# Two of four frame columns turned by VectorE by way of memory, and a pooled split kept back until the next pair of products

## Chip, cores and metric

The kernel runs on one core of one Trainium2 chip. The metric is its time on the device in microseconds (us), lower is better; the time before is the median of three executions. One more execution was taken with the hardware profiler, and all rows below are from it.

The core's engines run side by side, each through its own list of instructions in order: TensorE (PE in the rows; PEld is its weight load) multiplies, VectorE (DVE) and ScalarE (ACT) work element by element, GpSimd (POOL) does small things and issues some of the transfers (DMAs), SyncE (SP) issues most of them. They wait for each other through semaphores. An instruction that waits holds up all that stand behind it in its engine's list.

## What is computed

One layer over 2048 prompt frames and 32 sample frames of 1024 channels, cut to what matters here:

```python
hn = rmsnorm(h, g_mix)
proj = hn @ w_in                                     # 1024 x 3072
hA, bA, cA, zA, vB, zB = jnp.split(proj, ...)        # 512 columns each
u = cA * hA
yA = bA * (causal depthwise conv of u, width 3, + bias) * silu(zA)
yB = ((trailing mean of vB over 2/4/8/16 frames - vB) @ pool_w) * pool_scale * silu(zB)
h = h + concat(yA, yB) @ w_out
h = h + (p @ w_ple) * sigmoid(rmsnorm(h, g_ple) @ w_ple_gate)
return rmsnorm(h, g_final), ...
```

The change lies in the first two lines: in how the normalized frames hn are brought into the layout that the product with w_in needs, and in one step of yB.

## The kernel before

**Products.** Each float32 operand is split into two parts (`split`, L76: ScalarE casts the high part, VectorE subtracts it to get the low part), and a product takes three matmuls per block of 128 channels: high x high, high x low, low x high. The third needs the low half of the weight.

**Frames and groups.** The 2080 frames are five blocks of 416 (`NB`). `GROUPS` puts blocks 0 and 1 in group 0, 2 and 3 in group 1, block 4 in group 2. For groups 0 and 1 the product with w_in is done in seven half products in place of eight (`seven`, L894, and `pair`, L854): sums and differences of frames, called 11, 21, T1, T2, T3, 22 and T4, against sums and differences of weights, called 11, 12, S2, S1, S3, S4 and 22. A *product* below is one of these seven, 12 matmuls of 128 x 416.

**Units and pairs.** A *unit* is a group and one of four slices j of the 512 columns. From unit 1 of group 0 on a unit has three *pairs* of kinds of columns, zb with v, c with h, za with b, of seven products each, in the order 11, 12, S2, S1, S3, S4, 22. Three PSUM banks X, Y, Z belong to a pair (rows name them x_ch, y_ch, z_ch and so on). Between products ScalarE copies a bank out (`carry`, L866: into zs, V, c_s, U) or VectorE adds it (`out`, L869), and the next product into that bank waits for it. Weight tiles (`wtile`) have seven buffers, so a pair's weights are split while the pair before is multiplied. VectorE does the low half of each.

**Pooling.** When a zb/v pair is done, `v_first` (L908) copies the last bank into V and calls `pool_blocks` (L730): VectorE forms windowed sums (win) and pl, then the pooled frames are split into pp at L759. `mix` (L718) multiplies pp by the pool weights (pm) behind the c/h pair; in unit 0 of group 1, where two pairs run side by side, within the third pair.

**Frames of group 1.** While group 0's units 1 to 3 run, `next_columns` (L1038) prepares group 1's frames beside them, in the steps of a generator. Four columns c are done in the order 3, 0, 1, 2: columns 0 to 2 are two tiles of 128 frames (one of each block), column 3 is one tile of 64 (32 of each block). For a column `frame_sums` (L436) does this: the sum of squares of each tile (`sumsq`, ScalarE, rows "junk"; POOL makes rstd of it), `normal` (L404, VectorE scales a tile in one operation of 1024), `turn` (L410, four TensorE transposes for each half of each tile into a PSUM bank, rows pt_g), two copies by ScalarE (f12, f21), four subtractions by VectorE, seven splits, each into a *staged tile*, which POOL's queue writes to memory (`to_memory`, L482; p_d). Group 1 reads them back with `load_group`.

**Buffers.** Loaded frame tiles (xt), staged tiles and, where used, the tiles xs and xb named next come from one pool, `xin`, of five buffers of 4 KB a partition, so a load may wait until an older tile has been written out.

**The way through memory.** Block 4 is prepared in group 1 by `last_block` (L1050) without TensorE: `scaled_to_memory` (L1082) scales a tile in four operations of 256 columns into xs and writes it to xs_d, `from_memory` (L1093) loads it back as four pieces into xb, so that each 32 frames by 32 channels stand together, and `turned_in_place` (L1101) turns 32 x 32 blocks in one VectorE operation.

**What sets the order.** A scheduler orders each engine's instructions when the program is built, by its own estimate of times; `keep_in_program_order` binds some of them to the order of the source. `at_pace` (L1106) spreads the steps of a generator over the calls of `aside`, one after each product: 39 steps over 62 calls here.

Of the kernel before, what the change touches and what calls it, by code (L numbers as in the profile page):

```python
# [9 lines left out]
F32 = mybir.dt.float32  # L10
F32R = mybir.dt.float32r
AF = mybir.ActivationFunctionType
ALU = mybir.AluOpType
# [15 lines left out]
KH = KC // 2  # L29
EARLY = 3  # L30
LATE = 2


@with_exitstack
def trunk(ctx, tc, x_p, x_s, c_conv, c_pool, p_p, p_s, g_mix, w_in, conv_w, conv_b, pool_w,
# [294 lines left out]
    with ExitStack() as s1:  # L330
# [140 lines left out]
            yield  # L471


        NAMES = ("11", "21", "T2", "T1", "T3", "22", "T4")
        SLOTS = (("11", "21"), ("T2", "T1"), ("T3", "22"))
        p_d = {q: tc.dram_tile([P, KH, 2, NB], F32, name=f"p_d{q}") for q in NAMES}
# [4 lines left out]

        def to_memory(mem, name, src, at, n, t=None, later=False):  # L482
            t = t or staged(name)[:, :, :, :n]
            ins = put(t, src)
            if later:
                tc.keep_in_program_order(ins)
            nc.gpsimd.dma_start(mem[:, :, :, at:at + n], t.bitcast(F32))
# [185 lines left out]
        class Unit:  # L673
# [53 lines left out]
                nc.vector.scalar_tensor_tensor(z, pm[:, :NB], pscale(j), z, op0=ALU.mult, op1=ALU.mult)  # L727
                self.store(4 + j, b, self.zs)

            def pool_blocks(self, *bs):  # L730

                tb, j, V, L = self.tbs[bs[0]], self.j, self.V, self.L
                win = 2 << j
                if self.pooled is None:
                    self.pooled = wk.tile([P, 2, 2 * NB], F32R, tag="pp", bufs=1, name=f"pp_{self.tag}")
                for seg in self.segs(*bs):
                    lo, hi, at, new = seg
                    m = hi - lo
                    v = self.place(V, 15, seg)

                    src, off = V, (L + 15 if new else 0) + 15 + at
                    step, need = 1, win - 2
                    while step < win:
                        dst = etile(f"win{step}_{self.tag}_{tb}_{new}", 2 * NB + 16)
                        nc.vector.tensor_tensor(dst[:, :m + need], src[:, off - need:off + m],
                                                src[:, off - need - step:off + m - step], op=ALU.add)
                        src, off = dst, need
                        step *= 2
                        need -= step
                    pl = etile(f"pl_{self.tag}_{tb}_{new}", m)  # L750
                    skip = 0
                    if tb == 0:
                        skip = win - 1
                        nc.vector.tensor_tensor(pl[:, :skip], src[:, :skip], cnt[:, first_of(j):first_of(j + 1)],
                                                op=ALU.mult)
                        nc.vector.tensor_tensor(pl[:, :skip], pl[:, :skip], v[:, :skip], op=ALU.subtract)
                    nc.vector.scalar_tensor_tensor(pl[:, skip:], src[:, skip:m], 1.0 / win, v[:, skip:],
                                                   op0=ALU.mult, op1=ALU.subtract)
                    split(self.pooled[:, 0, lo:hi], self.pooled[:, 1, lo:hi], pl)  # L759

            def conv(self, *bs):

# [131 lines left out]
            def seven(self, B, aside, both=False):  # L894
# [12 lines left out]

                def v_first(ps):  # L908
                    nc.scalar.copy(at(V, 15, 0), ps)
                    self.pool_blocks(0, 1)  # L910
                    self.keep(V, 15, halo_v)

                def h_second(ps):
# [19 lines left out]
                def b_first(ps):  # L933
                    mul(self.cols(c_s, 0), ps, self.cols(c_s, 0))
                    self.store(j, 0, c_s)

                ring = [spare_ring if both and i == 1 else raw_ring for i in range(3)]
                pairs = [
                    ("zb", "v", B, {(0, 0): self.cols(zs, 0), (0, 1): self.cols(zs, 1), (1, 1): at(V, 15, 1)},
# [8 lines left out]
                while i < 3:  # L948
                    side_by_side = 2 if both and i == 0 else 1
                    if i <= 1 < i + side_by_side:  # L950
                        self.history(U, 2, halo_u, hist_u(j))
                    steps = [self.pair(*pairs[i + n], ring[i + n], ftile if n else None) for n in range(side_by_side)]
                    for n in range(8):
                        for st in steps:
                            next(st)
                            aside()
                        if both and i == 2 and n == 3:
                            for b in range(2):
                                self.mix(b)
                    for st in steps:  # L960
                        assert next(st, None) is None
                    i += side_by_side
                    if i - side_by_side <= 1 < i and not both:
                        for b in range(2):
                            self.mix(b)
# [72 lines left out]
        def next_columns(*cs):  # L1038

            load_ahead(1, cs[0])  # L1040
            for c, after in zip(cs, cs[1:] + (None,)):

                places = iter(t[:, :, :, i * DEC:(i + 1) * DEC] for t in map(staged, ("short_0", "short_1")) for i in range(4))
                dst = lambda q, src, n: to_memory(p_d[q], f"{q}_1_{c}", src, c * P, n, next(places) if n == DEC else None, True)
                for i, _ in enumerate(frame_sums(ahead.pop((1, c)), f"g1_{c}", dst)):
                    if after is not None and i in (6, 7):
                        load_half_ahead(after)
                    yield

# [27 lines left out]
                    back[c], m = from_memory(c * P, n), n  # L1077
                yield

        xs_d = tc.dram_tile([NB, D], F32, name="xs_d")  # L1080

        def scaled_to_memory(x, r):  # L1082

# [35 lines left out]
        for gi, tbs in enumerate(GROUPS):  # L1119
# [17 lines left out]
            for j in range(4):  # L1137
                unit = gi * 4 + j
                u = Unit(gi, tbs, j)
                if unit == 0:  # L1140
# [1 line left out]
                    B0["T4"] = piece_of(seventh("B0_T4"), 0)  # L1142
                    nc.sync.dma_start(B0["T4"].bitcast(F32), p_d["T4"])
                    p_d["T4"] = tc.dram_tile([P, KH, 2, NB], F32, name="p_dT4b")
                    aside = at_pace(next_columns(3, 0, 1, 2), 39, 62)
                elif gi == 0:
                    u.seven(B, aside)
                elif gi == 1:
# [444 lines left out]
```

## Time and profile before

| What | us |
|---|---|
| median of 3 executions | 927.71 (926.48 to 930.38) |
| the profiled execution, its own time | 928.9 |
| span of its profile | 927.1 |
| TensorE busy | 906.4 (98%) |
| VectorE busy | 722.5 (78%) |
| ScalarE busy | 475.7 (51%) |
| granted TensorE clock, mean | 0.997 |

How to read the rows. A row of the order of time has its start in us from the start of the span, its length in us, engine, line of the kernel, operation, output<-inputs by the program's names (buffer numbers left out), shape and how many like it were merged; in brackets at the end stands how long the engine was idle ahead of it and whose end released it. An instruction's length reaches up to 0.1 us past the start of the next, so prices are taken from start to start. A unit of group 0 takes some 50 us: unit 1 begins at 75.7, unit 2 at 127.3, unit 3 at 182.5, group 1 at 233.8.

### The profile page before, as it was taken

To read this page: it belongs to the slowest core of one execution; us is meant where nothing else is said; L and a number is where in the kernel's file an instruction comes from. 1 tells how busy PE (TensorE), PEld (TensorE's weight loads), DVE (VectorE), ACT (ScalarE), POOL (GpSimd) and SP (SyncE) were. 2 spreads that over 40 slices of the span, in tenths; PEclk is the share of its full clock that TensorE was granted. 3 is DMA by queue.
4 is the path that set the end of the run, shared out by engine and by line. 5 is a ranking of instruction groups with operands and counts; after the bars stand their busy time and mean duration, and the time that the engine had idled before them with its cause. 6 is when DMAs were issued, how large, how long until landed. Compare 5 with 4: busy or idle time off the path is not lost. (4 is left out here: it accounts for less than half of the span.)

```text
span 927.1 us, 12920 instructions
## 1 busy us (share of the span) xinstructions
PE 906.4 (98%) x4479; PEld 817.4 (88%) x4479; DVE 722.5 (78%) x1225; ACT 475.7 (51%) x880; POOL 153.1 (17%) x276
## 2 busy tenths in 40 slices
PE   7999998999999999999999999999999999999996
PEld 5999998999999999999999987888877868888884
DVE  6996998899488989785777678665554799888965
ACT  7743555464345555443545456334334776465554
POOL 4110311212000111000000010111111002333324
PEclk9999999999999999999999999999999999999998
DMA  8344654859955745458665359765785886799882
GB/s 261 91 141 144 188 173 141 246 160 318 413 163 175 198 155 163 119 184 279 180 186 172 128 192 282 251 202 171 245 230 160 299 251 163 187 230 236 224 244 92
DMA packets 140654, 186.37 MB, mean 201 GB/s; under 512 B 12044, under 2 KB 111244, under 8 KB 139309
## 3 DMA queue, kind: packets, MB, share of 16 engines
q1 hardware_dynamic: 120093, 126.07, 44.5%
q0 software_dynamic: 17760, 53.97, 19.8%
q10 hardware_dynamic: 2736, 5.51, 1.8%
q8 instruction: 35, 0.57, 0.3%
q14 instruction: 30, 0.25, 0.1%
HBM read 128.93 MB, written 56.56 MB: 200 GB/s over the span
## 5 line engine op out<-in xcount | busy, mean ns | idle before, releaser
L77 ACT CAST y_S<-y_fS 128x512 fp32r<-128x512 f32 x32 | 19.5, 621 | 42.4 <-PE x_o L167 17.4
L102 PE MATMUL e<-wq,pps 128*128 128x512 f32 (+1 forms) x156 | 38.9, 399 | 0.2 <-ACT pps L77 0.2
L69 POOL TENSOR_SCALAR ms_x<-ssq_x 128x1 f32<-128x1 f32 (+2 forms) x18 | 12.8, 710 | 143.9 <-ACT junk L88 143.6
L167 PE MATMUL x_o<-wo_b,y_S 128*128 128x512 f32 x128 | 35.8, 392 | 0.0
L563 PE MATMUL x_ch<-B,w_ch_S 128*128 128x416 f32 x168 | 34.6, 352 | 1.2 <-ACT c_s L866 1.2
L167 PE MATMUL x_g<-wg_b,g_S 128*128 128x512 f32 x128 | 35.7, 389 | 0.0
L563 PE MATMUL x_zab<-B,w_zab_S 128*128 128x416 f32 x168 | 34.3, 352 | 0.7 <-ACT V L866 0.7
L563 PE MATMUL x_zbv<-B,w_zbv_S 128*128 128x416 f32 x168 | 34.3, 352 | 0.3 <-ACT zs L866 0.3
L563 PE MATMUL z_zbv<-B,w_zbv_S 128*128 128x416 f32 x168 | 34.0, 351 | 0.0
L563 PE MATMUL z_ch<-B,w_ch_S 128*128 128x416 f32 x168 | 34.0, 351 | 0.0
L563 PE MATMUL z_zab<-B,w_zab_S 128*128 128x416 f32 x168 | 34.0, 351 | 0.0
L1382 POOL DMA_DIRECT2D e<-h_d x28 | 24.9, 909 | 53.4 <-DVE e L1379 46.4
L102 PEld LDWEIGHTS e<-wq,pps 128*128 128x128 f32 (+1 forms) x156 | 27.4, 182 | 6.9 <-ACT pps L77 0.5
L563 PEld LDWEIGHTS x_ch<-B,w_ch_S 128*128 128x128 f32 x168 | 31.2, 188 | 1.9 <-ACT c_s L866 1.6
L563 PEld LDWEIGHTS x_zab<-B,w_zab_S 128*128 128x128 f32 x168 | 31.3, 188 | 1.4 <-ACT V L866 1.0
L563 PEld LDWEIGHTS x_zbv<-B,w_zbv_S 128*128 128x128 f32 x168 | 31.2, 188 | 1.1 <-ACT zs L866 0.7
L563 PEld LDWEIGHTS z_ch<-B,w_ch_S 128*128 128x128 f32 x168 | 31.4, 188 | 0.3
L563 PEld LDWEIGHTS z_zab<-B,w_zab_S 128*128 128x128 f32 x168 | 31.4, 188 | 0.3
L563 PEld LDWEIGHTS z_zbv<-B,w_zbv_S 128*128 128x128 f32 x168 | 31.4, 188 | 0.3
L77 ACT CAST y<-y 128x512 fp32r<-128x512 f32 x24 | 14.8, 618 | 28.6 <-PE x_o L167 14.0
L77 ACT CAST g_S<-g_fS 128x512 fp32r<-128x512 f32 x32 | 19.0, 618 | 19.0 <-DVE g_fS L1501 12.3
L167 PEld LDWEIGHTS x_o<-wo_b,y_S 128*128 128x128 f32 x128 | 23.9, 188 | 5.1 <-ACT c_o L1185 0.3
(582 smaller groups left out, 2649.9 us busy)
## 6 DMA issues: line engine op xcount, KB each, us to landing
y<-y_d SPq DMA_DIRECT2D x16, 512.0 KB, 6.2
x<-in_x_prompt_dram SPq DMA_DIRECT2D x16, 512.0 KB, 5.5
h_d<-x SPq DMA_DIRECT2D x16, 512.0 KB, 2.6
hn<-h_d SPq DMA_DIRECT2D x61, 128.0 KB, 6.1
xt<-in_x_prompt_dram SPq DMA_DIRECT2D x15, 512.0 KB, 5.8
e<-e_d SPq DMA_DIRECT2D x15, 512.0 KB, 5.7
e<-h_d POOLq DMA_DIRECT2D x28, 256.0 KB, 6.4
out_dram<-e POOLq DMA_DIRECT2D x14, 512.0 KB, 4.2
```

The costliest lines, as they stand in the source:

```text
L69: nc.gpsimd.tensor_scalar(ms[:n], ssq[:n], scalar1=1.0 / D, scalar2=EPS, op0=ALU.mult, op1=ALU.add)
L77: ins = nc.scalar.copy(hi, src)
L102: nc.tensor.matmul(ps[:n], pps[:, a, k, :n], wp[k][b][:, cs], start=k + q == 0, stop=k == 1 and q == 2)
L167: nc.tensor.matmul(ps[:n], lhs[:, k, a, :n], w[b][:, k], start=start and k + q == 0, stop=k == KH - 1 and q == 2, skip_group_check=True)
L563: nc.tensor.matmul(ps[:, :NB], lhs[:, k, x], b[:, k, y], start=start and k + q == 0, stop=stop and k == KH - 1 and q == 2, skip_group_chec ...
L1382: nc.gpsimd.dma_start(ee, h_d[r:r + P, at[1] * NH:at[1] * NH + NH], accum_op=ALU.add)
```

## The change

Columns 3 and 0 of group 1 go through memory and are turned by VectorE (`frame_blocks`, new); columns 1 and 2 stay with `frame_sums`. For a column of two tiles frame_blocks has eleven steps where frame_sums has ten, so the pace is 41 over 62, and the load of the next column is asked for two steps later (one for column 3). The differences are formed from the turned tiles in SBUF, without ScalarE's two copies. xs_d grows from one block to four.

The second edit: `v_first` hands a list to pool_blocks, and the split of the pooled frames into pp is left in it. It is done in the pair behind, after that pair's fifth step (`LATER`; after the first step of the third pair in unit 0 of group 1), in program order. All units that use `seven` do this, those of group 1 too.

```diff
+LATER = 4
+IN_BLOCKS = 3, 0
...
+        whole = lambda t: t.rearrange("p k (g t) -> p k g t", t=32)
+
+        def frame_blocks(xs, tag, rows, dst):
+            xs = [x_stat(x, True) for x in xs]
+            yield
+            for x, r in zip(xs, rows):
+                scaled_to_memory(x, r)
+                yield
+            ts = [from_memory(r, x[1]) for x, r in zip(xs, rows)]
+            yield
+            n = P if len(xs) == 2 else DEC
+            f1, f2, f3, f4 = (whole(ftile(f"f{c}_{tag}")[:, :, :n]) for c in range(1, 5))
+            sub = lambda o, x, y: nc.vector.tensor_tensor(o, x, y, op=ALU.subtract)
+            u = turned_in_place(ts[0])
+            p11, p21 = u[:, :KH, :n // DEC], u[:, KH:, :n // DEC]
+            dst("11", p11, n)
+            yield
+            if len(xs) == 2:
+                u = turned_in_place(ts[1])
+            else:
+                u = u[:, :, 1:]
+            p12, p22 = u[:, :KH], u[:, KH:]
+            sub(f1, p12, p11)
+            dst("T1", f1, n)
+            yield
+            sub(f2, p22, f1)
+            sub(f3, p22, p12)
+            dst("21", p21, n)
+            yield
+            sub(f4, p21, f2)
+            dst("22", p22, n)
+            yield
+            dst("T2", f2, n)
+            yield
+            dst("T3", f3, n)
+            yield
+            dst("T4", f4, n)
+            yield
...
         def to_memory(mem, name, src, at, n, t=None, later=False):
             t = t or staged(name)[:, :, :, :n]
-            ins = put(t, src)
+            v = whole if len(src.shape) == 4 else lambda a: a
+            ins = split(v(t[:, :, 0]), v(t[:, :, 1]), src)
...
-            def pool_blocks(self, *bs):
+            def pool_blocks(self, *bs, late=None):
...
-                    split(self.pooled[:, 0, lo:hi], self.pooled[:, 1, lo:hi], pl)
+                    parts = self.pooled[:, 0, lo:hi], self.pooled[:, 1, lo:hi], pl
+                    if late is None:
+                        split(*parts)
+                    else:
+                        late.append(parts)
...
-                    self.pool_blocks(0, 1)
+                    self.pool_blocks(0, 1, late=late)
...
+                late = []
...
+                        if n == (0 if both else LATER):
+                            while i and late:
+                                tc.keep_in_program_order(split(*late.pop()))
...
-                for i, _ in enumerate(frame_sums(ahead.pop((1, c)), f"g1_{c}", dst)):
-                    if after is not None and i in (6, 7):
+                rows = (NB + c * P, 2 * NB + c * P) if c < 3 else (3 * NB,)
+                steps, loads = (frame_blocks(ahead.pop((1, c)), f"g1_{c}", rows, dst), (6 + len(rows), 7 + len(rows))) \
+                    if c in IN_BLOCKS else (frame_sums(ahead.pop((1, c)), f"g1_{c}", dst), (6, 7))
+                for i, _ in enumerate(steps):
+                    if after is not None and i in loads:
                         load_half_ahead(after)
                     yield
...
-        xs_d = tc.dram_tile([NB, D], F32, name="xs_d")
+        xs_d = tc.dram_tile([4 * NB, D], F32, name="xs_d")
...
-                    aside = at_pace(next_columns(3, 0, 1, 2), 39, 62)
+                    aside = at_pace(next_columns(3, 0, 1, 2), 41, 62)
```

## The prediction

> **What bounds the kernel now.** I read the page first, then busy time by windows, then the order of time on TensorE in the stretch that the change touches, then the engines that TensorE waits for there.
>
> ```profile
> span 927.1 us, 12920 instructions
> PE 906.4 (98%) x4479; PEld 817.4 (88%) x4479; DVE 722.5 (78%) x1225; ACT 475.7 (51%) x880; POOL 153.1 (17%) x276
> ```
>
> TensorE is busy for 98% of the span, so what counts is its work and the 20 us in which it stands. Group 0's units 1 to 3, in windows (busy PE, PEld, DVE, ACT, POOL, then clock, DMA share, GB/s):
>
> ```profile
> 50.00:100.00 50.00, 50.00 (x268) 48.82 (x267) 41.19 (x84) 21.55 (x45) 6.08 (x9) 1.00 0.52 148
> 100.00:150.00 50.00, 50.00 (x273) 49.35 (x272) 44.18 (x73) 26.86 (x51) 12.09 (x14) 1.00 0.67 207
> 150.00:200.00 50.00, 45.98 (x248) 43.43 (x247) 44.71 (x76) 27.02 (x50) 11.33 (x16) 1.00 0.55 165
> ```
>
> TensorE stands for 4 us between 150 and 200. VectorE is busy for 88 to 89% of 100:200: it has the least room of all the others. TensorE in order of time, through units 1 to 3:
>
> ```profile
> 82.48 2.43 PE L563 MATMUL z_zbv<-B,w_zbv_S 128*128 128x416 f32 x12
> 84.84 0.46 PE L415 MATMUL pt_g<-ident,xt 64*128 64x64 f32 x4
> ...
> 87.60 2.43 PE L563 MATMUL z_zbv<-B,w_zbv_S 128*128 128x416 f32 x12
> ...
> 116.51 2.44 PE L563 MATMUL z_zab<-B,w_zab_S 128*128 128x416 f32 x12
> 118.79 1.04 PE L415 MATMUL pt_g<-ident,xt 128*128 128x128 f32 x8
> ...
> 121.93 2.43 PE L563 MATMUL z_zab<-B,w_zab_S 128*128 128x416 f32 x12
> ...
> 138.70 2.43 PE L563 MATMUL z_zbv<-B,w_zbv_S 128*128 128x416 f32 x12
> 140.97 2.43 PE L563 MATMUL x_zbv<-B_T,w_zbv 128*128 128x416 f32 x12
> ...
> 150.03 2.43 PE L563 MATMUL z_ch<-B,w_ch_S 128*128 128x416 f32 x12
> 153.68 1.22 PE L563 MATMUL x_ch<-B,w_ch_S 128*128 128x416 f32 x5 [1.21 <-ACT c_s L866]
> 156.06 0.63 PE L415 MATMUL pt_g<-ident,xt 128*128 128x128 f32 x4 [1.16 <-DVE xt L406]
> ...
> 158.07 0.63 PE L415 MATMUL pt_g<-ident,xt 128*128 128x128 f32 x4 [0.62 <-DVE xt L406]
> ...
> 182.51 2.43 PE L563 MATMUL x_zbv<-B,w_zbv 128*128 128x416 f32 x12
> ```
>
> A product of 12 matmuls starts 2.27 us after the one before it (138.70 to 140.97); one matmul is 0.189. Eight transposes cost 0.88 (116.51 to 121.93, less two products), four short ones 0.58 (82.48 to 87.60, likewise). From 150.03 to unit 3's first product at 182.51 lie eleven products (25.0), six mix matmuls (1.1) and 16 transposes (1.8): 27.9 us of work in 32.5. **In this stretch 4.6 us are lost**, first to ScalarE's late copy of c_s, then to the scaled frames xt of column 1. On ScalarE:
>
> ```profile
> 151.29 0.89 ACT L77 CAST pp<-pl 128x832 fp32r<-128x832 f32 x1 [2.65 <-DVE pl L756]
> ...
> 153.14 0.48 ACT L866 COPY c_s<-x_ch 128x416 f32<-128x416 f32 x1
> ```
>
> The copy stood behind the pooled split (pp), which waited 2.65 us for VectorE. The second edit moves that split behind the copies of c_s and U.
>
> **The change, part by part.**
>
> *TensorE* loses column 0's 16 transposes and column 3's eight short ones: 2 x 0.88 + 2 x 0.58. **Term 1: -2.9 us**, all of it on the path, for TensorE does not stand there.
>
> *VectorE's prices* come from rows of the old way and from the last block, which goes through memory already:
>
> ```profile
> 128.45 1.28 DVE L448 TENSOR_TENSOR f_g<-pt_g,f_g 128x512 f32<-128x512 f32 x2
> 129.64 0.68 DVE L78 TENSOR_TENSOR 21_1_0_1375<-pt_g,21_1_0_1375 128x512 fp32r<-128x512 f32 x1
> ...
> 167.81 1.08 DVE L768 SCALAR_TENSOR_TENSOR c_s<-U,vec,c_s 128x832 f32<-128x832 f32 x1
> 168.89 0.65 DVE L727 SCALAR_TENSOR_TENSOR zs<-pm,vec,zs 128x416 f32<-128x416 f32 x1
> ...
> 181.60 1.28 DVE L406 SCALAR_TENSOR_TENSOR xt<-xt,rstd_x,g_bc 128x1024 f32<-128x1024 f32 x1 [1.01 <-POOL rstd_x L73]
> ...
> 303.25 0.58 DVE L869 TENSOR_TENSOR c_s<-y_ch,c_s 128x416 f32<-128x416 f32 x1
> 303.75 1.02 DVE L78 TENSOR_TENSOR pp<-pl,pp 128x832 fp32r<-128x832 f32 x1
> 304.68 1.24 DVE L1103 STREAM_TRANSPOSE xb<-xb 128x1024 f32<-128x1024 f32 x1
> 305.84 1.64 DVE L1089 SCALAR_TENSOR_TENSOR xs<-xt,rstd_x,g_bc 128x256 f32<-128x256 f32 x4
> ```
>
> From start to start: 0.60 for 128x512, 0.50 for 416 columns, 0.93 for 832, 1.16 for a turn of 1024; four scalings of 256 take about 1.6 where one of 1024 takes 1.2. So column 0 costs VectorE 2 x (0.4 + 1.16) = 3.1 us more, column 3 some 0.4 + 0.6 = 1.0. The four subtractions and seven splits stay; ScalarE loses four copies, an engine that is half idle in all three windows. Column 3's turn is not yet on the path: its weights wait in buffers ahead of TensorE, so I set it at nothing. If its frames came back from memory some 3 us late, the same VectorE queue would hold the copies that free unit 1's banks, and the price would be those 3 us.
>
> *The way through memory* adds three writes on POOL's queue and twelve loads on SP's, ahead of raw_zbv_2a (column 3) and raw_zab_2a (column 0). Sizes and us to landing, from the DMA view of two windows:
>
> ```profile
> p_d<-11_1_0_1300 POOLq DMA_DIRECT2D x1, 512.0 KB, 3.9
> raw_zab_2a<-in_w_in_dram SPq DMA_DIRECT2D x1, 512.0 KB, 4.1
> p_d<-21_1_0_1375 POOLq DMA_DIRECT2D x1, 512.0 KB, 6.8
> ...
> p_d<-21_1_1_1725 POOLq DMA_DIRECT2D x1, 512.0 KB, 7.7
> ...
> xs_d<-xs POOLq DMA_DIRECT2D x3, 512.0 KB, 3.0
> xb<-xs_d SPq DMA_DIRECT2D x12, 128.0 KB, 5.3
> ```
>
> With 3.0 out, 5.3 back and some 2 for issuing, a tile is away for about 10 us. By a count of VectorE's operations column 0's scalings end near 118 and 119, and its turns stand in the order behind bank copies of unit 2 that cannot come before 130 and 135. They are covered. raw_zab_2a, now behind the eight loads of column 0, is still some 10 us ahead of its first use.
>
> *What the new order puts on the path.* In the order that the scheduler makes of the changed program, column 0's differences and six of its seven splits come in one run around the seam between unit 2's first two pairs; the old way spread them over the unit. Frame tiles, staged tiles, xs and xb share five buffers. In the changed program the second load of column 1 takes the buffer of staged tile 21, so it waits until that tile is in memory. ScalarE's square sum of that load stands ahead of its copy of U (unit 2's z_ch), and TensorE's z_ch waits for that copy. VectorE's scaling of the same load stands ahead of all of unit 2's za/b weights. I follow that chain with the old clock, TensorE 2.9 us ahead:
>
> - z_zbv (138.70 + 2.43) ends at 138.2. VectorE then adds to zs (0.5) and does f2, T1, f3 and the split of 21: the last starts at 140.5.
> - The write of 21 was issued 0.98 us after its split began (129.64 above to 130.62 below) and took 6.8: landed at 148.3.
> - The load of a frame tile at that place: issues on SP and the square sums on ScalarE that wait for them,
>
> ```profile
> 130.62 0.85 POOL L487 DMA_DIRECT2D p_d<-21_1_0_1375  x1 [1.94 <-DVE 21_1_0_1375 L78]
> ...
> 165.59 0.59 SPq L392 DMA_DIRECT2D xt<-in_x_prompt_dram  x1
> ...
> 171.83 0.34 SPq L392 DMA_DIRECT2D xt<-in_x_prompt_dram  x1
> ...
> 173.06 1.06 ACT L88 ACTIVATE junk<-xt 128x1024 bf16<-128x1024 f32 x1 [2.59 <-DMA xt<-in_x_prompt_dram]
> ...
> 179.50 1.06 ACT L88 ACTIVATE junk<-xt 128x1024 bf16<-128x1024 f32 x1 [2.90 <-DMA xt<-in_x_prompt_dram]
> ```
>
>  7.5 and 7.7 us. I take 7.5: the square sum starts at 155.9, the copy of U follows 1.05 later (as c_s at 153.14 above), TensorE goes on near 157.5. Without waits it would be there at 150.3: 152.3 as the place of x_ch's fifth product, less 2.9, and five matmuls that the scheduler put in between. **Term 2: +7.2 us.**
> - The scaling starts 2.1 after the square sum (179.50 to 181.60) and ends at 159.2. Up to the low half of za's first weight VectorE then has pp (0.93), ten of 128x512 (6.0), four adds and products of 416 columns (2.0), two mix products (1.2), two taps (2.0) and a wait of 0.4 for x_ch's end: 171.7. TensorE reaches that weight at 167.3 (z_ch and x_ch 6.4, 16 transposes 1.8, mix 1.3, from 157.5). **Term 3: +4.4 us.**
> - Two short waits for U and V behind it: **term 4: +0.5**. The old losses of this stretch go: **term 5: -4.6**.
>
> Sum: -2.9 + 7.2 + 4.4 + 0.5 - 4.6 = **+4.6 us**. After unit 3 no row of the profile gives it back: behind it TensorE runs without a gap through 200:300. The split moved in group 1 I set at nothing, since units there keep their mix behind the second pair; its bounds are 0.3 either way, about one bank wait.
>
> Bounds. Terms 2 and 3 hang on two transfers: 6.8 lies between 3.9 and 7.7 in the rows, 7.5 between 4.1 and 7.7, nearest to the frame loads at this very place. High end: +1.1. Low end: 6.3 us earlier, and there VectorE's own work takes over. From 138.2 to the end of that scaling it has 14.2 us of operations by the prices above, so without any wait it is there at 152.4, 6.8 us earlier; term 2 then vanishes, term 3 is 4.8, and the sum is about -2.2.
>
> The Trainium skill, "DMA: Bandwidth & Descriptors", section "Anatomy of one DMA — SWDGE (gpsimd) path", gives about 2.0 us plus bytes at 436 GB/s for one transfer, an estimate of 3.2 us for 512 KB. By it both transfers together would be about 8 us shorter and the sum would fall to the low end, 925.5. The rows of this stretch, 6.8 and 7.5, say otherwise, so it stays a rival.
>
> **The rivals.**
>
> A. *The loads are not late, VectorE's queue alone decides*: the sum is -2.2, 925.5. For it: writes of 3.9 and loads of 4.1 stand in the rows. Against it: the writes of 21 took 6.8 and 7.7 in two of three columns, with other tiles on the queue, and four now go out closer together.
>
> B. *Faster in full*: both terms vanish, -2.9 - 4.6 = -7.5, 920.2. Its mechanism is the second edit: with pp off ScalarE's way c_s and U are copied at once. Its place is x_ch's fifth product, and it decides if za's first weight is ready by 160.1. By the rows VectorE is 4.8 us too slow for that even without waits.
>
> C. *More than the forecast*: column 3's or column 0's frames return late, and VectorE, in order, stands at a turn ahead of the bank copies. Price: 3 to 6 us on top, 937. For it: SP issues the loads behind weight loads that wait for buffers. Against it: 5 us of room at both turns.
>
> **How the numbers follow.** The profiled execution took 928.9 (span 927.1 and 1.8 around it), 1.2 above the median of 927.71. With +4.6 it would be 933.5; against the median **932.5 us**. Chances: forecast 0.60 (its own range 929 to 936), A 0.20, B 0.10, C 0.10. The range 924 to 938 holds the forecast, A and most of C. A measurement here tells about 0.5% (4.6 us) from no change, and the forecast lies on that line: 0.38 of its 0.60 is slower and 0.22 same. Faster 0.10 (B), same 0.42 (A and 0.22), slower 0.48.
>
> **What would show it.** Right: transposes pt_g x32 instead of x56, and no loss of TensorE before 145; then two gaps in unit 2, one of 5 to 8 us at x_ch's and z_ch's last products, named by ScalarE's U or c_s behind a square sum that waits for DMA, one of 3 to 5 us at x_zab, named by VectorE's w_zab; unit 3 begins near 187. Wrong: TensorE without a gap from 145 to 165 (B); only the second gap (A); a gap in unit 1 or at unit 2's first pair, with VectorE idle ahead of a turn for xb (C).

## The result, and the profile after

The changed kernel takes 936.27 us (median of six executions, 935.25 to 937.25). The kernel before, executed beside it, takes 928.5 (926.48 to 930.55). The ratio is 1.0082, with a 95% interval of 1.0068 to 1.0096: the change makes the kernel slower by 0.8%. The forecast was 932.5 with a range of 924 to 938; the measured time lies inside that range, and 0.3 us above the forecast's own 929 to 936.

The page of the changed kernel, its span and the busy time of each engine (its own time was 937.25):

```profile
span 935.4 us, 12912 instructions
PE 907.1 (97%) x4455; PEld 819.5 (88%) x4455; DVE 726.9 (78%) x1237; ACT 477.3 (51%) x876; POOL 154.7 (17%) x279
```

The transposes are gone (24 matmuls fewer), and yet TensorE's busy time did not fall. The windows show why (busy PE, PEld, DVE, ACT, POOL, clock, DMA share, GB/s):

```profile
100.00:150.00 50.00, 49.46 (x262) 48.62 (x261) 43.25 (x77) 27.17 (x51) 11.38 (x16) 1.00 0.66 198
150.00:200.00 50.00, 39.76 (x191) 37.89 (x192) 42.08 (x68) 23.49 (x43) 10.29 (x15) 0.86 0.66 197
```

Between 150 and 200 TensorE stands for 10.2 us, not 4.0, and its granted clock is 0.86, not 1.00. Busy time at a lower clock is longer busy time. TensorE in order of time:

```profile
124.37 2.43 PE L610 MATMUL x_zbv<-B,w_zbv 128*128 128x416 f32 x12
...
150.79 0.65 PE L610 MATMUL x_ch<-B,w_ch_S 128*128 128x416 f32 x2 [1.33 <-ACT c_s L917]
...
157.07 1.06 PE L610 MATMUL z_ch<-B,w_ch_S 128*128 128x416 f32 x2 [5.07 <-ACT U L917]
157.93 3.54 PE L610 MATMUL x_ch<-B,w_ch_S 128*128 128x416 f32 x10
...
173.42 3.83 PE L610 MATMUL x_zab<-B,w_zab 128*128 128x416 f32 x10 [4.38 <-DVE w_zab L80]
...
190.82 2.43 PE L610 MATMUL x_zbv<-B,w_zbv 128*128 128x416 f32 x12
```

Unit 2 begins 2.9 us earlier than before (124.37, before 127.28), unit 3 begins 8.3 later (190.82, before 182.51), which is the whole difference of the two spans. Between them lie what I call the first gap (1.33 for c_s and 5.07 for U) and the second gap (4.38 for w_zab). Of the old waits of this stretch only the one for c_s is left. The ten matmuls of x_ch from 157.93 to 161.31 take 0.34 us each and the ten of x_zab from 173.42 to 177.05 take 0.36, not 0.189.

What stood ahead of those copies and weights, from the order of time on POOL, SP, ScalarE and VectorE (rows of several engines, put together by start):

```profile
141.53 0.85 POOL L534 DMA_DIRECT2D p_d<-21_1_0_1407  x1 [0.34 <-DVE 21_1_0_1407 L80]
...
142.47 5.86 SPq L394 DMA_DIRECT2D xt<-in_x_prompt_dram  x2
...
155.48 1.06 ACT L90 ACTIVATE junk<-xt 128x1024 bf16<-128x1024 f32 x1 [4.74 <-DMA xt<-in_x_prompt_dram]
...
156.53 0.49 ACT L917 COPY U<-z_ch 128x416 f32<-128x416 f32 x1
...
157.59 1.28 DVE L408 SCALAR_TENSOR_TENSOR xt<-xt,rstd_x,g_bc 128x1024 f32<-128x1024 f32 x1 [4.13 <-POOL rstd_x L75]
...
161.51 0.59 DVE L920 TENSOR_TENSOR U<-x_ch,U 128x416 f32<-128x416 f32 x1 [1.70 <-PE x_ch L610]
...
172.69 1.28 DVE L80 TENSOR_TENSOR w_zab<-raw_zab_2a,w_zab 128x512 fp32r<-128x512 f32 x2
```

The write of staged tile 21 is issued at 141.53 and lands 6.4 us later, at 147.9. The SPq row is two loads in one: the second of them, column 1's second load, is issued at 147.99, as soon as that write has landed. The square sum that waits for it starts at 155.48 (forecast 155.9), U is copied behind it, and VectorE, which stood for 4.13 us, scales that tile from 157.59. Up to here this is the forecast's chain, row by row. (The 1.33 us for c_s come from column 1's first load in the same way, its square sum at 148.47; they add nothing, for TensorE would have waited for U all the same.) VectorE then waits 1.70 us for the end of x_ch, whose matmuls are slow, where the forecast has 0.4, and comes to za's first low halves at 172.69. What the forecast lacked is the clock. The windows view, in steps of 3.4 us laid so that a change of clock falls on a border:

```profile
151.00:154.40 3.40, 1.01 (x5) 0.65 (x4) 2.46 (x4) 0.00 (x0) 0.89 (x1) 0.99 1.01 283
154.40:157.80 3.40, 0.73 (x2) 0.71 (x3) 0.21 (x1) 2.32 (x4) 0.74 (x2) 0.50 0.94 274
157.80:161.20 3.40, 3.40 (x11) 3.23 (x11) 2.00 (x2) 0.00 (x1) 0.00 (x0) 0.50 0.07 20
...
168.00:171.40 3.40, 1.04 (x8) 0.66 (x7) 3.40 (x5) 1.73 (x4) 0.84 (x1) 1.00 0.67 214
171.40:174.80 3.40, 1.38 (x4) 1.33 (x5) 3.40 (x7) 0.20 (x1) 0.85 (x1) 0.50 0.62 183
174.80:178.20 3.40, 3.40 (x12) 3.23 (x11) 3.40 (x7) 3.40 (x7) 0.00 (x0) 0.50 0.43 125
```

The first number behind the comma is TensorE's busy time, the 0.99 to 0.50 near the end of a line its clock. Twice the clock falls to half in the middle of a gap and stays there for 6.8 us, long after TensorE has work again. In the four half-clock windows TensorE is busy for 0.73 + 3.40 + 1.38 + 3.40 = 8.9 us. If half of that is lost, it is 4.5 us; by the rows of z_ch, x_ch, x_zab and y_zab behind the two gaps, against 0.189 us a matmul, it is 4.3.

### The profile page after: what moved, and what is told of

Read it like the earlier page. It is cut to its first block, busy times and chain, and to the rows that moved or that the text cites. A ratio compares the mean times of both kernels' runs of the same rounds, so it can differ in the third digit from the quotient of the medians.

```text
span 935.4 us, 12912 instructions
## 1 busy us (share of the span) xinstructions
PE 907.1 (97%) x4455; PEld 819.5 (88%) x4455; DVE 726.9 (78%) x1237; ACT 477.3 (51%) x876; POOL 154.7 (17%) x279
## 4 chain that ended last, share of the span: by engine, by line
PE 75%; DMA 4%; DVE 3%; issue 3%; ACT 1%; POOL 1%; POOLq 0%; DVEq 0%; ACTq 0%
PE x_g L169 9%; PE x_o L169 8%; PE x_zab L610 6%; PE x_ch L610 5%; PE x_zbv L610 5%; PE e L104 5%; PE z_g L169 4%; PE z_o L169 4%; PE z_zab L610 3%; PE z_ch L610 3%; PE z_zbv L610 2%; PE y_g L169 2%; PE y_o L169 2%; PE b L610 2%; PE za L610 2%
## 5 line engine op out<-in xcount | busy, mean ns | idle before, releaser
L169 PEld LDWEIGHTS x_g<-wg_b,g_S 128*128 128x128 f32 x128 | 24.0, 188 | 5.0
```

The costliest lines, as they stand in the source:

```text
L169: nc.tensor.matmul(ps[:n], lhs[:, k, a, :n], w[b][:, k], start=start and k + q == 0, stop=k == KH - 1 and q == 2, skip_group_check=True)
```

## The experiments

All times are medians, the ratio is to the kernel before executed on the same chip in turn. The last column is units 2 and 3 of group 0 in the profiled execution, from unit 2's first product to group 1's: it leaves out the program's start, which takes up to 2.8 us longer in some executions (unit 1 begins at 75.68 before, at 78.49 with column 3 alone).

| Kernel | us | ratio, 95% interval | units 2 and 3, us |
|---|---|---|---|
| before | 928.0 to 928.6 | | 106.5 |
| the change | 936.27 | 1.0082 (1.0068 to 1.0096) | 116.9 |
| second edit alone | 926.82 | 0.9982 (0.9970 to 0.9993) | 102.8 |
| column 3 alone | 928.34 | 1.0002 (0.9992 to 1.0011) | 104.1 |
| column 0 alone | 931.29 | 1.0031 (1.0017 to 1.0044) | 108.3 |
| without the second edit | 934.89 | 1.0078 (1.0065 to 1.0091) | 115.7 |
| column 2 alone | 942.00 | 1.0143 (1.0130 to 1.0156) | |
| loads two steps earlier | 931.37 | 1.0031 (1.0016 to 1.0046) | 111.7 |
| second gap filled | 936.22 | 1.0080 (1.0062 to 1.0097) | 115.0 |
| two low halves on GpSimd | 929.56 | 1.0013 (1.0005 to 1.0022) | 109.5 |
| loads three steps earlier, GpSimd | 931.23 | 1.0027 (1.0013 to 1.0042) | 110.9 |
| the same, eight low halves | 933.63 | 1.0062 (1.0046 to 1.0077) | 112.7 |
| za begun early, two steps | 932.69 | 1.0040 (1.0024 to 1.0057) | 114.8 |
| za begun early, three steps | 935.37 | 1.0077 (1.0062 to 1.0092) | 113.1 |

### The parts of the change alone

**The second edit alone:**

```diff
-IN_BLOCKS = 3, 0
+IN_BLOCKS = ()
-                    aside = at_pace(next_columns(3, 0, 1, 2), 41, 62)
+                    aside = at_pace(next_columns(3, 0, 1, 2), 39, 62)
```

> Only the second edit: all four columns turned by TensorE as before, pace 39 over 62, the pooled split kept back. My theory (the loss comes from column 0's way through memory, which makes the second load of column 1 late) says that this edit costs nothing and takes away the 1.2 us wait for c_s that the kernel before had: between -2 and 0 us against the kernel before. The rival that the kept-back split is the cause says at least +4 us. TensorE shows no gap over 1.5 us between 100 and 200.

Measured 926.82 us, 1.2 less than the kernel before (928.01). All of TensorE's waits between 75 and 240, from the view of waits:

```profile
PE x_ch L610 <- DVE U L920: 1.2, 1, 1.2
```

The wait for c_s is gone, as the theory has it. It is the fastest kernel of this study, and the interval over twelve executions leaves 1 out. Units 2 and 3 are even 3.7 us shorter than before in the profiled execution, but that is the slowest of the twelve (929.29), and its program's start is 2.4 us longer.

**Column 3 alone** (IN_BLOCKS = (3,), pace 40 over 62):

> Column 3 alone through memory (pace 40 over 62), with the kept-back split. Theory: one transpose run of 0.58 us goes, nothing late, so between -2.5 and 0 us against the kernel before. Rival (column 3's turn is to blame): +3 us or more, with a gap of TensorE in unit 1 or at unit 2's first pair.

Measured 928.34: as the kernel before, 0.3 us above the theory's upper end. No long gap came, but beside the second edit alone it is 1.5 us slower although TensorE has 1.2 us less to do: two runs of four short transposes are gone, of which the expectation counts one, and unit 1 takes 50.4 us, there 51.6. In the profiled execution unit 3 is 1.4 us longer than there, 0.8 of it a new wait for VectorE's V; in unit 2 a wait of 0.6 for VectorE stands in place of the 1.2 for U. Where the rest of the gain went is not shown.

**Column 0 alone** (IN_BLOCKS = (0,), pace 40 over 62):

> Column 0 alone through memory (pace 40 over 62), with the kept-back split; the second load of column 1 waits for the write of staged tile 21 here too. Theory: the whole loss is here, +6 to +9 us against the kernel before (936.27 less the 0.58 us of column 3's transposes that stay, within 2), with a gap of 4 us or more in unit 2's c/h pair and a granted clock under 0.92 in 150:200. Rival (both columns together overload VectorE): +0 to +3.

Measured 931.29, +3.3 us: less than the theory's +6 to +9 and 0.3 above the rival's range, so it fits the rival (it takes both columns) better. Rows of ScalarE, TensorE and VectorE:

```profile
148.42 1.06 ACT L90 ACTIVATE junk<-xt 128x1024 bf16<-128x1024 f32 x1 [2.66 <-DMA xt<-in_x_prompt_dram]
...
156.30 1.06 ACT L90 ACTIVATE junk<-xt 128x1024 bf16<-128x1024 f32 x1 [4.23 <-DMA xt<-in_x_prompt_dram]
...
151.08 4.53 PE L610 MATMUL x_ch<-B,w_ch_S 128*128 128x416 f32 x12 [3.02 <-ACT c_s L917]
...
163.09 1.29 DVE L80 TENSOR_TENSOR w_zab<-raw_zab_2a,w_zab 128x512 fp32r<-128x512 f32 x2
```

The second load waits for the write of 21 here too (5.3 us on SP's queue; the square sum at 156.30 is 28.9 us behind unit 2's first product, in the changed kernel 31.1). But here the first copy of c_s stands behind the first load's square sum (148.42), in the changed kernel the second copy, and TensorE met that: a gap of 3.0 us at 148, with a halved clock behind it. At half clock two products filled the time until the second load was there, and no gap came for it. VectorE does za's low halves at 163.09 instead of 172.69, ahead of column 1's staged tiles, and no second gap came either. So column 0 costs some 3 us by itself, and the rest of the 8 comes only with both columns. The rows put it down to the other order on ScalarE and VectorE; no run changes that order alone.

**Without the second edit:**

```diff
-                    self.pool_blocks(0, 1, late=late)
+                    self.pool_blocks(0, 1)
```

> The changed kernel without its second edit: columns 3 and 0 go through memory, the pooled split is done at once as before. Theory (the second edit is worth about the 1.7 us that it gained alone, and the late load costs the rest): 936 to 940 us. Rival (the second edit, together with column 0, is what puts U behind the square sum): under 933 us.

Measured 934.89, between the two ranges, nearer to the theory's. The waits of unit 2:

```profile
PE pt_g L417 <- DVE xt L408: 6.3, 1, 6.3
PE x_zab L610 <- DVE w_zab L80: 4.2, 1, 4.2
```

The two gaps have the same size, 6.3 and 4.2, but TensorE now stands at a transpose for the scaled tile, not at z_ch for U. So the first gap is that load, whatever instruction meets it first, and the second edit, which alone is worth 1.2 us, is worth nothing here.

**Column 2 alone** (IN_BLOCKS = (2,), pace 40 over 62):

> Column 2 alone through memory (pace 40 over 62), with the kept-back split. No load follows this column, so no buffer of its staged tiles delays one. Theory: 16 transposes (1.8 us) go and no gap over 1.5 us comes: 923 to 926 us, under the 926.8 of the second edit alone. Rival (VectorE's longer queue in unit 3 makes weights late wherever a column goes through memory): 928 us or more, with a gap of 2 us or more between 180 and 235.

Measured 942.0: the rival, and more. The two long waits, and the row of VectorE behind which the first of them stands:

```profile
PE x_zab L610 <- ACT V L917: 5.4, 1, 5.4
PE x_zab L610 <- DVE w_zab L80: 5.0, 1, 5.0
```

```profile
229.13 0.69 DVE L588 TENSOR_TENSOR s_ch<-raw_ch_0b 128x512 f32<-128x512 f32 x1 [7.41 <-DMA raw_ch_0b<-in_w_in_dram]
```

No load of frames follows column 2, and yet unit 3 has a gap of 5.0 us at the same weight, from 215.6 to 220.6. From 205 to 220.5 VectorE is busy for all 15.5 us: its queue alone suffices for it. The other gap is again an instruction early in the order that waits for a load, here the weight sum s_ch of the next unit; unit 3's own S2 weights stood behind it for 7.41 us.

### The late load

**Loads two steps earlier.** Nothing is taken out and no work is moved off an engine; only the place in the buffers' order changes.

```diff
-                steps, loads = (frame_blocks(ahead.pop((1, c)), f"g1_{c}", rows, dst), (6 + len(rows), 7 + len(rows))) \
+                steps, loads = (frame_blocks(ahead.pop((1, c)), f"g1_{c}", rows, dst), (4 + len(rows), 5 + len(rows))) \
```

> The changed kernel, with the two loads of the next column asked for two steps earlier behind a column that goes through memory; nothing else. The second load of column 1 then takes a buffer that is free when the split of tile 22 is done, at about 142.5, not when the write of tile 21 has landed, at 148. Theory: it lands 5 to 6 us earlier, the first gap (6.4 us) shrinks to 2 us or less, TensorE keeps its clock there, the second gap stays between 2 and 5 us: 927 to 931 us, 5 to 9 less than the changed kernel. Rival A (VectorE's added work alone sets the time): not under 934, with the second gap grown to 8 us or more. Rival (SP's other loads, which now stand behind a waiting load, come late): 936 or more, with a new gap named by a weight tile.

Measured 931.37, 4.9 less than the change, 0.4 above the theory's range. The two long waits of units 1 to 3, and rows of ScalarE and TensorE:

```profile
PE x_zab L610 <- DVE w_zab L80: 4.4, 1, 4.4
PE x_ch L610 <- ACT c_s L917: 2.3, 1, 2.3
```

```profile
148.09 0.62 ACT L79 CAST T<-f_g 128x512 fp32r<-128x512 f32 x1 [0.58 <-DMA p_d<-21_1_0_1407]
149.81 1.06 ACT L90 ACTIVATE junk<-xt 128x1024 bf16<-128x1024 f32 x1 [1.09 <-DMA xt<-in_x_prompt_dram]
...
151.31 0.62 ACT L79 CAST T<-f_g 128x512 fp32r<-128x512 f32 x1 [0.35 <-DMA p_d<-22_1_0_1448]
...
152.39 4.08 PE L610 MATMUL x_ch<-B,w_ch_S 128*128 128x416 f32 x12 [2.26 <-ACT c_s L917]
```

The load is issued at 144.08, behind the split of 22 and no longer behind the write of 21. The square sum starts 5.7 us earlier (149.81) and the first gap falls from 6.4 to 2.3. That it is not zero has two causes in these rows, all ahead of the copy of c_s at 151.84: the load still comes 1.09 late, and casts into staged tiles wait for the writes of 21 and 22. TensorE did not keep its clock, against the theory: the twelve matmuls behind the gap take 3.9 us, not 2.27. The second gap is 4.4 as before, although the scaling came earlier: then it is not the load that sets its size. VectorE is busy for 14.2 of the 15.5 us from 154 to its end.

### The clock

**The second gap filled with work:**

```diff
+                if (self.gi, self.j, ka) == (0, 2, "za"):
+                    for _ in range(22):
+                        (nc.tensor.matmul(Z[:, :NB], pw[:, 0, 0], B["11"][:, 0, 0], start=True, stop=True, skip_group_check=True))
                 half_product(X, make("S2"), B["T2"], False)
```

> The changed kernel with 22 more matmuls of 128 x 416 in TensorE's list, in unit 2 ahead of the ten matmuls of x_zab that wait for w_zab (into a bank that the next products begin anew). They are 4.2 us of extra work in a gap of 4.4 us, so nothing is done sooner but TensorE stands less. Theory (after a gap the clock is halved, and the halved stretch behind this gap costs 2.4 us): the granted clock stays 1.00 from 168 to 180, x_zab's ten matmuls take 1.9 us, not 3.6, and the time falls by 1.5 to 2.5 us to about 934. Rival (the slow matmuls behind the gap have another cause, such as late weights): the same or slower than the changed kernel, 936 to 938.

The windows, and TensorE's row behind the filler:

```profile
168.00:174.00 6.00, 6.00 (x37) 5.71 (x35) 6.00 (x10) 2.67 (x4) 0.84 (x1) 1.00 0.67 209
174.00:180.00 6.00, 5.40 (x29) 5.20 (x29) 6.00 (x12) 4.08 (x9) 0.84 (x1) 1.00 0.44 128
```

```profile
174.74 2.16 PE L610 MATMUL x_zab<-B,w_zab 128*128 128x416 f32 x10 [0.60 <-DVE w_zab L80]
```

The clock stays at 1.00, and x_zab's ten matmuls take 2.0 us (174.74 to 176.74) where they took 3.63. Unit 2, from its first product to unit 3's, is 64.3 us long instead of 66.4: 2.2 us shorter with 22 matmuls more. In both kernels x_zab goes on 49.05 us behind unit 2's first product, so nothing was done sooner, and all of the 2.2 us are saved behind the gap. So in this stretch the theory holds. The time of the whole kernel does not show it: 936.22 us, the rival's figure, with six executions from 932.78 to 938.94. In the profiled one, the slowest of the six, the program's start was 1.3 us longer and the part behind unit 3 2.7 longer; TensorE stood for 1.7 of these between 750 and 900, where the edit touches nothing. Why is open.

### VectorE's queue

**Two low halves on GpSimd** (with the loads two steps earlier):

```diff
-                put(t, src[q])
+                split(t[:, :, 0], t[:, :, 1], src[q], nc.gpsimd if (gi, j, ka) == (0, 2, "za") and q in ("11", "12") else nc.vector)
```

> The kernel with the loads two steps earlier, in which moreover the low halves of unit 2's first two za/b weights are subtracted by GpSimd, not VectorE. Theory (the second gap, 4.4 us, is VectorE's queue: its low half stands behind eight other operations that are not urgent): the gap shrinks to under 1 us, the halved clock behind it goes too (1.7 us), and the time falls from 931.4 to 925 to 927 us. Rival (the weights or their high halves are late, or GpSimd takes longer than VectorE's queue did): 930 us or more, with the gap now named by GpSimd's w_zab.

Measured 929.56, between the two ranges. The wait for w_zab is gone as the theory had it, but a new one of 2.6 us stands two products later, at the S2 weight, with the halved clock behind it; the first gap stays at 2.3:

```profile
PE x_zab L610 <- ACT w_zab_S L79: 2.6, 1, 2.6
```

That weight's difference (L585) is VectorE's too, and VectorE is busy for 14.8 of the 15 us from 155 to 170. The move also cost VectorE something. Its rows and GpSimd's:

```profile
143.29 1.02 DVE L792 TENSOR_TENSOR win<-win 128x836 f32<-128x836 f32 x1
...
146.74 2.14 DVE L792 TENSOR_TENSOR win<-win 128x832 f32<-128x832 f32 x1
...
146.70 1.30 POOL L80 TENSOR_TENSOR w_zab<-raw_zab_2a,w_zab 128x512 fp32r<-128x512 f32 x1 [1.10 <-ACT w_zab L79]
```

A window sum takes 1.02 alone and 2.14 beside GpSimd's subtraction. Each of the two moves saved VectorE 0.6 us; the first cost it 1.1 here, the second 0.8 at a low half of T, which took 1.45 and not 0.69.

**Loads three steps earlier, with the same two low halves on GpSimd** (`3 + len(rows), 4 + len(rows)` in the line of loads):

> As the run with two low halves on GpSimd, but the loads of the next column are asked for three steps earlier than in the changed kernel. The second load of column 1 then waits for the split of tile 21, not 22, and ScalarE's copy of c_s stands ahead of T4's, which waits for a write. Theory (what is left of the first gap, 2.3 us, is ScalarE behind that load and the writes of 21 and 22): the first gap falls under 1.2 us; the gap at the S2 weight (2.6 us, VectorE's queue) and the halved clock behind it (1.6 us) stay: 926.5 to 928.5 us. Rival (the load is late wherever it stands, because the way back through memory crowds the queues): 929 us or more with the first gap at 2 us or more.

Measured 931.23: the rival's time. The first gap was 1.9, between the theory's 1.2 and the rival's 2, and a wait of 1.0 for the scaled tile came behind it; the wait at S2 stayed (2.5).

**Six more low halves on GpSimd** (T3 and T4 of column 0, T1 to T4 of column 1; `on_pool` picks these names):

```diff
-            ins = split(v(t[:, :, 0]), v(t[:, :, 1]), src)
+            ins = split(v(t[:, :, 0]), v(t[:, :, 1]), src, nc.gpsimd if on_pool(name) else nc.vector)
```

> The same, and GpSimd also subtracts the low halves of the staged tiles T3 and T4 of column 0 and T1 to T4 of column 1: six operations of 0.6 us taken off VectorE in units 1 and 2. Theory (the loss is VectorE's and ScalarE's order around a late load, not the transposes that were saved): no gap over 1.2 us is left in unit 2, the clock stays at 1.00 there, and the gain of 2.9 us from the transposes shows: 923.5 to 926.5 us, faster than the kernel before (928.3) and than the second edit alone. Rival (GpSimd's 1.3 us per low half holds up its own writes to memory, and they the staged tiles): 927.5 us or more, with a gap named by a staged tile or a DMA.

Measured 933.63, the rival again, though not at a staged tile. TensorE stood for 4.5 us at a transpose, for the scaled tile xt, whose rstd came late. GpSimd's rows and VectorE's:

```profile
156.48 1.33 POOL L80 TENSOR_TENSOR T<-f_g,T 128x512 fp32r<-128x512 f32 x1
157.70 1.43 POOL L75 TENSOR_TENSOR rstd_x<-ms_x,nhalf 128x1 f32<-128x1 f32 x1
...
156.16 2.54 DVE L80 TENSOR_TENSOR pp<-pl,pp 128x832 fp32r<-128x832 f32 x1
159.16 1.29 DVE L408 SCALAR_TENSOR_TENSOR xt<-xt,rstd_x,g_bc 128x1024 f32<-128x1024 f32 x1 [0.46 <-POOL rstd_x L75]
```

The tiny rstd, on which the frames hang, stands behind the subtractions that were moved, and pp's subtraction takes 2.54 instead of 1.02 beside them. GpSimd is busy for only 18% of this kernel's span, but it is no free engine here.

**za/b begun early.** VectorE's order is changed without GpSimd: the za/b pair of unit 2 is begun after the c/h pair's fifth step, and its first two weights are made there.

```diff
+                if (self.gi, self.j, ka) == (0, 2, "za"):
+                    ready, late_make = {q: make(q) for q in ('11', '12')}, make
+                    make = lambda q: ready[q] if q in ready else late_make(q)
...
+                        if (self.gi, j, i, n) == (0, 2, 1, 4):
+                            early_pair = self.pair(*pairs[2], ring[2], None)
+                            next(early_pair)
...
```

(Left out at the dots: the lines that go on with this pair in its turn.)

With the loads two steps earlier:

> The changed kernel with the next column's loads asked for two steps earlier and with unit 2's za/b pair begun before the c/h pair's last three weights are made, so that VectorE does the low halves of za's first two weights right behind the scaling of column 1's second tile, ahead of some dozen operations that stood before them. Nothing goes to GpSimd. Theory (the second gap is a matter of order on VectorE, not of its amount of work): no gap named by w_zab over 1.5 us is left, the first (c_s, about 2.3 us) stays, TensorE multiplies za's first products meanwhile: 925 to 928 us. Rival (VectorE's amount of work sets it, and what was moved back comes late instead): 929.5 us or more, with the lost time now at w_ch or another weight.

And three steps earlier:

> The same with the loads three steps earlier. Theory: as the run before, with the first gap between 1.5 and 2.5 us: 925 to 928.5 us, within 1.5 of the run with two steps. Rival: 929.5 us or more.

Measured 932.69 and 935.37: the rival's time in both. With two steps the wait at w_zab falls from 4.4 to 1.0, as the theory had it, and the one at c_s stays (2.2). But 3.7 us stand one unit later, at unit 3's first differences (with three steps 2.4 at w_zab and 2.4 there):

```profile
PE x_zbv L610 <- ACT w_zbv_S L79: 3.7, 1, 3.7
```

ScalarE and VectorE ahead of that weight, with two steps:

```profile
185.47 1.06 ACT L90 ACTIVATE junk<-xt 128x1024 bf16<-128x1024 f32 x1 [3.17 <-DMA xt<-in_x_prompt_dram]
...
187.10 0.59 DVE L954 TENSOR_TENSOR c_s<-c_s,V 128x416 f32<-128x416 f32 x1 [2.82 <-ACT V L980]
```

This is the first gap's chain again, one column later. Column 2's second load waited 7.1 us on SP's queue for the write of one of column 1's staged tiles. ScalarE's square sum waited for that load, ScalarE's V stands behind the square sum, and VectorE stood for that V (2.82 us, with three steps 1.77) ahead of the difference that unit 3 needs. So these two runs gave the rival's time, but do not show its cause: a late load set most of the new gap, not VectorE's amount of work. That the second gap itself is VectorE's amount of work is read from its full queue there (14.2 of 15.5 us, above) and in column 2 alone; no run takes enough work off VectorE, without a price elsewhere, to test it.

## Why the prediction was right, and what it lacked

**Direction and range.** Slower was forecast, and slower it is. But 936.27 lies outside the forecast's own 929 to 936, and the wider range holds it only because its upper end was drawn for rival C, of which nothing happened. That the time lies in the range is in part luck.

**The buffer and the late load.** Right in each step: 21's write issued at 141.53 (forecast 141.5), the square sum at 155.48 (155.9), TensorE going on at 157.07 (157.5). The run with earlier loads shows that it is this wait for the write: without it the square sum comes 5.7 us sooner, and the first gap falls by 4.1 us.

**Term 1**, -2.9 us: measured -2.9 at unit 2's start.

**Term 2**, +7.2: the two waits of the first gap are 1.33 + 5.07 = 6.4. Counted as the prediction does, from the place without waits (150.24) to 157.07, it is 6.8.

**Term 3**, +4.4: measured 4.38, and the close agreement is luck. Both ends of the gap came 1.7 us later than forecast: TensorE reached the weight at 169.04 (forecast 167.3), since x_ch had run at half clock, and went on at 173.42 (171.7), since VectorE had waited for that same x_ch. The prediction's own parts for TensorE's way, 6.4 + 1.8 + 1.3 from 157.5, moreover give 167.0, so that its term would be 4.7. Its cause was right only in part. I had VectorE's scaling of the late tile end at 159.2 and counted its work from there. The scaling ended as forecast, near 158.8, but with the load 5.7 us earlier the gap was the same 4.4, since TensorE then came earlier too; the prediction's low end has 4.8 for that case. Column 2 shows a gap of 5.0 at the same weight without a late frame load. So the load sets where the gap stands, and VectorE's whole queue how long it is: by the prediction's prices VectorE does 3.1 us more for column 0, in a stretch where it was busy for 88% before.

**Term 4**, +0.5 for short waits behind it: none came. **Term 5**, -4.6: the old losses are gone.

**The step that failed** is the premise "I follow that chain with the old clock". The forecast counts gaps of 7.2 and 4.4 us and lets TensorE go on at full speed behind them. Unit 3 begins at 190.82 where the forecast has 187.1 (182.51 + 4.6), 3.7 us later. Of these, 2.2 lie behind the second gap and are the halved clock: with the gap filled by idle work the clock stays at 1.00 and they are gone. Another 1.7 lie ahead of it, at VectorE's wait for the slow x_ch; that they are the halved clock behind the first gap is read from the rows, for no run fills that gap. Term 4 gives 0.5 back, and 0.3 are left open. Counted by terms it is the same: as measured they sum to -2.9 + 6.4 + 4.4 + 0 - 4.6 = +3.3 us, the span grew by 8.3, and 4.3 to 4.5 of the missing 5.0 are matmuls at half clock; the rest stands mostly at the ends of rows ahead of the gaps. In units 1 to 3 of the kernel before no gap was longer than 1.2 us, and two at its program's start, of 2.4 and 2.3, left the clock at 1.00, so the rows of this stretch could not show it. One sign stood in the view before: in its last window, 850:928, in which TensorE runs out of work, the clock is 0.96.

The Trainium skill, "TensorE: Matmul & The Clock Gate", section "Part 1: The HAM clock gate (the "warmup" mystery)", says that TensorE's clock is halved after an idle window of about 3.4 us and restored after a busy one, and that these windows run freely. The trace agrees with the halved stretches of 3.4 and 6.8 us; the gate fell here in windows in which TensorE was not idle but worked for 1.0 us.

**Column 3's turn at nothing**: right for the changed kernel, which has no loss before 149. Alone it gave back its own 1.2 us and 1.5 more, in part by a wait for VectorE.

**Group 1's split at nothing, within 0.3**: from unit 3's first product to the end of the span both kernels take 744.6 us (935.4 - 190.82, before 927.1 - 182.51). In this, unit 3 is 0.8 us shorter and what follows 0.8 longer, with a new wait of 0.4 for pp in group 1. From group 1's first product on, the profiled executions of all kernels here take 692.5 to 696.5 us, so they do not resolve 0.3.

**Rival A**, VectorE's queue alone (925.5): its mechanism is real, its price was too low. With the loads mended the kernel is at 931.4, since the second gap brings its own halved clock (3.3 us are lost to it in that run, at both gaps) and the first does not vanish. **Rival B**, faster in full: its mechanism, pp off ScalarE's way, gives 1.2 us alone and nothing where the load is late. **Rival C**, frames back late: VectorE waited at no turn.

## What to carry to other kernels

Before work is taken off the engine that sets the pace, look at what the engines that receive it have left in that stretch: at 88% busy, a few us more and one stall came back as gaps of the first engine, and six attempts to mend them moved the gaps without removing them all. When buffers are shared, follow each load to the transfer that frees its buffer, since a load asked for one tile later can wait for a write of 6 to 7 us; an order that mends one gap can bring the next such load onto the path. And a gap of TensorE of two us or more can cost more than its length: where the clock fell behind it, the work lost 1.6 to 3 us more here.

## What the runs showed of the hardware

**Half clock comes in steps of 3.4 us, and a window need not be idle for it.** From two of the runs with two low halves on GpSimd and with earlier loads, windows of 3.4 us on the grid that the change of clock gives (TensorE's busy time is the first number behind the comma):

```profile
147.10:150.50 3.40, 2.35 (x13) 1.99 (x11) 3.40 (x6) 1.81 (x4) 2.45 (x3) 1.00 0.89 319
150.50:153.90 3.40, 2.13 (x11) 2.11 (x12) 3.12 (x4) 2.22 (x4) 3.25 (x5) 1.00 0.74 216
...
167.60:171.00 3.40, 1.14 (x4) 0.59 (x4) 3.40 (x7) 2.58 (x5) 1.01 (x2) 1.00 0.78 230
171.00:174.40 3.40, 3.24 (x10) 3.08 (x10) 3.37 (x7) 0.62 (x1) 0.67 (x1) 0.50 0.91 302
```

```profile
151.30:154.70 3.40, 1.50 (x8) 1.15 (x7) 2.99 (x7) 2.89 (x7) 1.63 (x2) 1.00 0.63 186
154.70:158.10 3.40, 3.40 (x14) 3.18 (x13) 1.68 (x2) 1.26 (x3) 3.25 (x4) 0.51 0.96 271
```

In the first run the gap of 2.3 us at 149.5 lies across a border, each window has over 2.1 us of work, and the clock stays. Its gap of 2.6 us at 167.3 lies, but for 0.3 us, in one window, which keeps 1.14 us of work, and the next window runs at half clock. In the second run 1.50 us of work were too little as well. With the loads two steps earlier and nothing on GpSimd, a gap of 2.3 us at the same copy of c_s left 1.14 us of work in its window, and the next ran at half clock. So the same gap costs its length alone or its length and 1.6 us more, by where it falls; executions of kernels with such gaps spread over up to 7 us (928.13 to 935.25 with za begun early), though that the phase is what spreads them was not tested.

**VectorE and GpSimd slow each other.** Beside a GpSimd subtraction of 1.30 us a VectorE operation took 2.14 instead of 1.02, and pp 2.54 instead of 1.02; GpSimd's rstd beside that pp took 1.43 instead of 0.55. The Trainium skill, "SBUF — State Buffer", section "SBUF: two separate sides", says that the two engines share a pair of ports that one instruction holds to its end, where VectorE's operation has two inputs in SBUF as these have; the trace agrees, as VectorE lost about as long as GpSimd worked.
